# First embedding stage of a two-layer decoder trunk: two of four gate units as block products, inside the first MLP's pool

## The chip, the core and the metric

The kernel runs on one core of one Trainium2 chip. The metric is the device time of one execution in microseconds (us). It is the median of 3 runs. One further execution was recorded by the hardware profiler; all rows of "the profile" and "the trace" in this text are from it. The engines are PE (TensorE, matrix products), PEld (its weight loads), DVE (VectorE), ACT (ScalarE), POOL (GpSimd) and SP (which issues DMAs). L12 is line 12 of the kernel.

## What is computed

Two decoder layers over 512 tokens of width 1024, all in float32: a mixer (attention with a short convolution in layer 0, gated linear attention in layer 1), a gated MLP with a causal convolution, and the per-layer embedding. The change is in the embedding of layer 0:

```python
def _per_layer_embedding(x, p_i, norm, w_gate, w_proj):
    gate = jax.nn.sigmoid(_rms_norm(x, norm) @ w_gate)   # (512, 1024) @ (1024, 1024)
    return gate * (p_i @ w_proj)                         # (512, 256) @ (256, 1024)

for i in range(DEPTH):
    ...
    x = x + _conv_ffn(_rms_norm(x, ffn_norm[i]), ...)
    x = x + _per_layer_embedding(x, p[i], ple_norm[i], ple_w_gate[i], ple_w_proj[i])
```

## The kernel before, in words

**Tiles.** The residual `xT` lies turned: 8 tiles of 128 features x 512 tokens. Every float32 operand is split into a high part in the reduced format of TensorE and a low part (the rest), and each product is three matmuls (`mm3`, L162 to L164): high x high, high x low, low x high. `split` (L109/L110, or L112/L113 with a gain) does this for an operand, `cut` (L142/L143) for weights: ACT writes the high part, DVE subtracts. `advance` (L264) makes the next operand of a tile: split by the gain, square (L275), add to the sum of squares (L276). `end_norm` turns that sum with four PE transposes (L329), and DVE (L331, L171) and POOL (L172) make 1/rms; `spread` (L341) turns it into `R`, one row of 512 tokens on all partitions.

**Block products.** `seven` (L857) computes 256 output columns for 512 tokens by seven block products of 256 tokens where the plain way takes eight (a Strassen-Winograd scheme). A product is 4 block rows x 3 matmuls of 256 columns (L872 to L874). It is a generator with four steps: W, then ACT copies it into the two result banks X and Y (L883, L884); V, X left and Y left, then a copy (L893); X right, then ACT copies X right into Y right (L897); Y right and X right again. Its weight forms are made by `first_forms` and `more_forms` (four DVE subtractions of 512 columns in the loaded weights) and four `cut_blocks` (L819/L820). Its operand forms are sums of blocks of an even and an odd tile; in the MLP `operand` (L783) makes them (L791 scales by the gain, L796, L797, L800, L801 are the sums, then two splits). `seven` serves the MLPs of both layers.

**The stage.** `ple0` (L1281) runs in a pool of its own after the MLP of layer 0. It has four units of two output tiles. A unit loads 1 MB of gate weights and 256 KB of projection weights (both through L119 on SP), computes two gates of 48 matmuls in all (8 inputs x 3, for each tile), then for the unit before it two projections of `p` (12 matmuls), and `finish`: DVE multiplies gate and projection (L1295), adds to `xT` (L1296), and `advance` makes the operand for the mixer of layer 1. The gate itself is DVE times `R` (L1314), ACT sigmoid (L1315). The transposes of `end_norm`, `spread` and `load_p` (L1275) stand among the matmuls of unit 0. Right after the stage come the value products of the mixer of layer 1 (`Values`, 368 columns wide), then its first `feature` products.

**What sets the order.** A planner fixes the instruction order of each engine ahead of time: among what is ready in its reckoning, the earliest in the program goes first. Inside a `manual_schedule` block the instructions of the named engine keep the order of the program; ones from outside may fall between. Each engine then runs its list in order, waiting on semaphores. A pool keeps a fixed number of buffers for each tag. The tiles of a tag get theirs in the order of the program, each the first that is free; a buffer is free when the last instruction that uses its tile is done. In the MLP's pool there are 2 buffers of tag `zt` (`both()`, two halves of 512 columns each), 7 of `four`, 3 of `z`; elsewhere 3 of `wh` and `wl` (cut weights), 2 of `raw` (loaded weights), 4 banks `ps` and 4 `pa` of PSUM. A pool that reuses the memory of a closed one waits for all of that one.

Of the kernel before, what the change touches and what calls it, by code (L numbers as in the profile page):

```python
# [9 lines left out]
F32 = mybir.dt.float32  # L10
# [3 lines left out]
AF = mybir.ActivationFunctionType  # L14
ALU = mybir.AluOpType
# [3 lines left out]
P = 128  # L19
S = 512  # L20
D = 1024
NT = S // P
ND = D // P
# [5 lines left out]
ET = mybir.EngineType  # L29
# [27 lines left out]
class Kernel:  # L57
# [229 lines left out]
    def blocks(self, m, gain, scratch, tags):  # L287


        nc = self.nc  # L290
        H = S // 2
        gx = scratch()
        nc.scalar.activation(gx, self.xT[m], AF.Copy, scale=gain[:, m : m + 1])

        def parts(x):
            w = x.shape[1]
            h, l = self.pair(self.fp, *tags)
            self.split((h[:, :w], l[:, :w]), x)
            return lambda b, c: (h[:, b * H + c * P : b * H + (c + 1) * P], l[:, b * H + c * P : b * H + (c + 1) * P])

        if m % 2 == 0:
            self.even = gx
            self.e1 = parts(gx[:, :H])
        else:
            e, o = self.even, gx
            op = parts(o)
            s12, s34 = scratch(), scratch()
            nc.vector.tensor_tensor(s12[:, :H], e[:, H:], o[:, H:], ALU.add)
            nc.vector.tensor_tensor(s12[:, H:], s12[:, :H], e[:, :H], ALU.subtract)
            s12p = parts(s12)  # L310
            nc.vector.tensor_tensor(s34[:, :H], e[:, :H], e[:, H:], ALU.subtract)
            nc.vector.tensor_tensor(s34[:, H:], o[:, :H], s12[:, H:], ALU.subtract)
# [22 lines left out]
    def spread(self):  # L335
# [7 lines left out]
        nc.scalar.copy(R, pr)  # L343
        return R

# [437 lines left out]
    def operand(self, m, gain, tags):  # L783


        nc, fp = self.nc, self.mlp
        H = S // 2
        if m % 2 == 0:
            self.scratch = self.four(fp, F32)
        x = self.scratch[:, m % 2]  # L790
        nc.scalar.activation(x, self.xT[m], AF.Copy, scale=gain[:, m : m + 1])  # L791
        self.xg.append(self.pair(self.fp, *tags))
        self.split(self.xg[m], x)
        if m % 2:
            e, o, s12, s34 = (self.scratch[:, u] for u in range(4))
            nc.vector.tensor_tensor(s12[:, :H], e[:, H:], o[:, H:], ALU.add)  # L796
            nc.vector.tensor_tensor(s12[:, H:], s12[:, :H], e[:, :H], ALU.subtract)  # L797
            out = self.four(fp)
            self.split((out[:, 0], out[:, 1]), s12)
            nc.vector.tensor_tensor(s34[:, :H], e[:, :H], e[:, H:], ALU.subtract)  # L800
            nc.vector.tensor_tensor(s34[:, H:], o[:, :H], s12[:, H:], ALU.subtract)  # L801
            self.split((out[:, 2], out[:, 3]), s34)
            self.forms.append([(out[:, q, c], out[:, q + 1, c]) for q in (0, 2) for c in (slice(0, H), slice(H, S))])
        self.squares(m)

    def by_parity(self, raw):

# [49 lines left out]
    def seven(self, od, ws, xg, forms, keep=True):  # L857

        nc = self.nc
        H = S // 2
        mm = nc.tensor.matmul
        W, V = self.pa(), self.pa()[:, :H]
        X, Y = self.ps(), self.ps()
        plain, t13, t2 = ws

        def product(out, w, c, x, first=False):
            kw = dict(skip_group_check=True)
            for j in range(ND // 2):  # L870
                (wh, wl), (xh, xl) = w(j, c), x(j)
                mm(out, wh, xh, start=first and j == 0, stop=False, **kw)  # L872
                mm(out, wh, xl, start=False, stop=False, **kw)  # L873
                mm(out, wl, xh, start=False, stop=j == ND // 2 - 1, **kw)  # L874

        def tokens(u, half):
            c = slice(half * H, (half + 1) * H)
            return lambda j: (xg[2 * j + u][0][:, c], xg[2 * j + u][1][:, c])

        s1, s2, s3, s4 = (lambda j, q=q: forms[j][q] for q in range(4))  # L880
        left, right = slice(0, H), slice(H, S)
        product(W[:, left], plain, 0, tokens(0, 0), True)
        nc.scalar.copy(X[:, left], W[:, left])  # L883
        nc.scalar.copy(Y[:, left], W[:, left])  # L884
        yield
        product(V, t13, 0, s1, True)
        more = V
        if keep:
            more = self.sp.tile([P, S], F32, tag="acc", name=self.nm("more"), bufs=1)[:, :H]
            nc.scalar.copy(more, V)  # L890
        product(X[:, left], plain, 1, tokens(1, 0))
        product(Y[:, left], t2, 0, s2)
        nc.scalar.copy(X[:, right], Y[:, left])  # L893
        yield
        last = self.cut_blocks(od)
        product(X[:, right], t13, 1, s3)
        nc.scalar.copy(Y[:, right], X[:, right])  # L897
        yield
        product(Y[:, left], last, 1, s4)
        product(X[:, right], last, 0, tokens(1, 1))  # L900
        yield X, Y, more

    def ffn(self, i, project, next_gain):


        nc, a, tc = self.nc, self.a, self.tc
        gain = self.g_ffn[i]
        wu = a["ffn_w_up"][i].rearrange("(k p) n -> p k n", p=P)
        w0, w1, w2, bb = self.fcv

        mine, other = (("a0", "a1"), ("b0", "b1"))[:: 1 - 2 * i]
        with tc.tile_pool(name=f"ffn{i}", bufs=1) as fp:
# [4 lines left out]
            def both():  # L917
                return fp.tile([P, 2, S], F32, tag="zt", name=self.nm("zt"), bufs=2)
# [108 lines left out]
            xg = self.xg  # L1027
# [7 lines left out]
            steps, w1c, w0c = ready  # L1035
            with tc.manual_schedule(engines={ET.PE}):
                late = begin(0, steps, w1c)
                for d in range(groups):
                    g, y = both(), both()
# [7 lines left out]
                    if d == 0:  # L1047
                        R = self.spread()
                    X, Y, more = next(steps)
                    rest = late  # L1050

                    if d + 1 < groups:
                        steps, w1c, w0c = prepare(d + 1)
                        late = begin(d + 1, steps, w1c)
# [8 lines left out]
                    if 4 <= d < groups - 1:  # L1063
                        split_one(d - 4)
            self.begin_norm(mine)
            finish = lambda m: self.advance(m, next_gain)
            if i == 1:
                self.forms = []
                halves = []

                def half():
                    if not halves:
                        x = both()
                        halves.extend([x[:, 0], x[:, 1]])
                    return halves.pop(0)

                self.half = half
                finish = lambda m: self.blocks(m, next_gain, half, mine if m < 4 else other)
            work = [lambda f=f: split_blocks(f) for f in (14, 16, 18, 20)]
            for f in (8, 10, 12):  # L1080
                split_pair(f)
            self.down(i, acts, down_forms, both, work, finish)
            if i == 0:
                self.end_norm()
            else:
                self.ple1(fp)

    def down(self, i, acts, forms, both, work, finish):

# [188 lines left out]
            out.append(hl)  # L1278
        return out

    def ple0(self, next_gain):  # L1281
        nc, a = self.nc, self.a
        with self.tc.tile_pool(name="ple0", bufs=1) as pool:
            xg, R, pT = self.xg, None, None
            wg = a["ple_w_gate"][0].rearrange("(k p) n -> p k n", p=P)
            wp = a["ple_w_proj"][0].rearrange("(k p) n -> p k n", p=P)
            self.begin_norm(("b0", "b1"))

            def finish(m2, w, gates):
                for c in range(2):  # L1290
                    m, s = m2 + c, gates[c]
                    pj = self.ps()
                    for k in range(2):
                        self.mm3(pj, w(k, c * P, (c + 1) * P), pT[k], start=k == 0, stop=k == 1)
                    nc.vector.tensor_tensor(s, s, pj, ALU.mult)  # L1295
                    nc.vector.tensor_tensor(self.xT[m], self.xT[m], s, ALU.add)  # L1296
                    self.advance(m, next_gain)

            late = None
            for m2 in range(0, ND, 2):  # L1300
                g = self.weights(wg[:, :, m2 * P : (m2 + 2) * P], ND, 256)
                w = self.weights(wp[:, :, m2 * P : (m2 + 2) * P], 2, 256)
                gates = []
                for c in range(2):
                    pg = self.ps()
                    for k in range(ND):
                        self.mm3(pg, g(k, c * P, (c + 1) * P), xg[k], start=k == 0, stop=k == ND - 1)
                    gates.append(pg)
                if R is None:
                    R = self.spread()  # L1310
                    pT = self.load_p(0, pool)
                for c in range(2):
                    s = pool.tile([P, S], F32, tag="pg", name=self.nm("pg"), bufs=4)
                    nc.vector.tensor_tensor(s, gates[c], R, ALU.mult)  # L1314
                    nc.scalar.activation(s, s, AF.Sigmoid)  # L1315
                    gates[c] = s
                if late:
                    finish(*late)
                late = (m2, w, gates)
            finish(*late)  # L1320
            self.end_norm()

    def ple1(self, fp):
# [611 lines left out]
    def run(self):  # L1935
        self.setup()
        self.ffn(0, self.mixer0(), self.g_ple[0])
        self.ple0(self.g_mix[1])
        self.ffn(1, self.mixer1(), self.g_ple[1])


# [29 lines left out]
```

## Time and profile before

| | |
|---|---|
| median of 3 runs | 1207.76 us (1206.56 to 1208.12) |
| profiled execution | 1206.43 us, span 1204.7 us |
| busy share of the span | PE 99%, PEld 86%, DVE 80%, ACT 55%, POOL 4% |
| the stage on PE | 525.41 us (first gate matmul) to 581.68 us (first value matmul) |
| granted clock | 1.0 |

The busy share is that of all instructions of an engine in the span. A matmul's record overlaps the next one, so the pace of PE is read from the starts of consecutive rows, not from durations. Where a row of the timeline ends in brackets, the engine sat idle before it, and the arrow names what released it. A row with xN merges N instructions.

### The profile page before, as it was taken

Reading aid. Unit: us, or ns where it says so; the run is one execution under the profiler, and the core shown is the slowest. Engines: PE = TensorE matmul, PEld = TensorE weight load, DVE = VectorE, ACT = ScalarE, POOL = GpSimd, SP = SyncE. Lnnn points to the kernel's source line nnn. Section 1 sums busy time; section 2 is a strip of 40 time slices with the busy share of each in tenths; the row PEclk is TensorE's granted clock in tenths of the full one; section 3 lists DMA queues with packets and bytes.
Section 4 is the critical chain, followed back from the end, with each engine's and each line's share of the span. In section 5 each row is a group of like instructions: output and inputs, shape, how many; then the busy total and the mean of one; then the engine's idle time right before and its main releaser. Section 6 shows DMA issues by size and latency. Waiting matters only on the chain.

```text
span 1204.7 us, 17692 instructions
## 1 busy us (share of the span) xinstructions
PE 1197.7 (99%) x7013; PEld 1036.9 (86%) x7013; DVE 968.3 (80%) x1527; ACT 665.3 (55%) x1081; POOL 43.8 (4%) x64
## 2 busy tenths in 40 slices
PE   9999999999999999999999999999999999999998
PEld 8877788999899889888988988889998899888887
DVE  6786587899998986746579876677999999988595
ACT  7466455656555644534573564555565645646374
POOL 2600000000000000000100000000000000000000
PEclk9999999999999999999999999999999999999999
DMA  7321322423333242222322222313242423322501
GB/s 222 93 85 45 96 74 70 140 71 108 103 106 104 91 137 97 96 89 94 115 93 68 73 70 71 105 49 127 70 141 70 136 75 120 134 88 97 210 1 70
DMA packets 111127, 117.61 MB, mean 98 GB/s; under 512 B 2840, under 2 KB 106322, under 8 KB 111044
## 3 DMA queue, kind: packets, MB, share of 16 engines
q1 hardware_dynamic: 109680, 115.35, 29.2%
q8 instruction: 55, 0.90, 0.3%
q0 software_dynamic: 560, 0.42, 0.3%
q10 hardware_dynamic: 804, 0.70, 0.2%
q14 instruction: 28, 0.23, 0.1%
HBM read 114.37 MB, written 2.10 MB: 97 GB/s over the span
## 4 chain that ended last, share of the span: by engine, by line
PE 87%; DVE 8%; ACT 2%; issue 1%; POOL 1%; DMA 0%; ACTq 0%; DVEq 0%; POOLq 0%
PE ps L162 12%; PE ps L163 12%; PE ps L164 12%; PE pa L163 7%; PE pa L162 7%; PE pa L164 7%; PE ps L872 5%; PE ps L874 5%; PE ps L873 5%; PE pa L872 2%; PE pa L874 2%; PE pa L873 2%; DVE wl L143 2%; PE ps L1371 1%; PE ps L1369 1%
## 5 line engine op out<-in xcount | busy, mean ns | idle before, releaser
L142 ACT ACTIVATE wh<-raw 128x1024 fp32r<-128x1024 f32 (+4 forms) x154 | 152.4, 991 | 155.1 <-PE ps L163 109.4
L143 DVE TENSOR_TENSOR wl<-raw,wh 128x1024 fp32r<-128x1024 f32 (+4 forms) x154 | 175.6, 1142 | 50.1 <-ACT wh L142 49.7
L819 ACT ACTIVATE wh<-raw 128x1024 fp32r<-128x1024 f32 x78 | 82.8, 1061 | 118.4 <-DVE raw L844 65.2
L932 DVE SCALAR_TENSOR_TENSOR zt<-z,vfa,zt 128x510 f32<-128x510 f32 (+1 forms) x176 | 130.6, 744 | 11.7 <-ACT zt L930 11.2
L820 DVE TENSOR_TENSOR wl<-raw,wh 128x1024 fp32r<-128x1024 f32 x78 | 95.3, 1222 | 19.3 <-ACT wh L819 19.2
L930 ACT ACTIVATE zt<-z,vfb 128x512 f32<-128x512 f32 x88 | 71.1, 810 | 28.9 <-DVE four L983 12.8
L162 PE MATMUL ps<-b,wh 128*128 128x512 f32 x192 | 76.8, 400 | 0.0
L163 PE MATMUL ps<-b,wh 128*128 128x512 f32 x192 | 75.1, 391 | 0.0
L164 PE MATMUL ps<-b,wl 128*128 128x512 f32 x192 | 75.0, 391 | 0.0
L163 PE MATMUL pa<-b,wh 128*128 128x512 f32 x176 | 69.0, 392 | 0.0
L163 PE MATMUL pa<-a,wh 128*128 128x512 f32 x176 | 69.0, 392 | 0.0
L162 PE MATMUL pa<-a,wh 128*128 128x512 f32 x176 | 69.0, 392 | 0.0
L162 PE MATMUL pa<-b,wh 128*128 128x512 f32 x176 | 69.0, 392 | 0.0
L164 PE MATMUL pa<-a,wl 128*128 128x512 f32 x176 | 68.4, 389 | 0.0
L164 PE MATMUL pa<-b,wl 128*128 128x512 f32 x176 | 68.4, 389 | 0.0
L872 PE MATMUL ps<-four,wh 128*128 128x256 f32 x232 | 65.1, 281 | 0.5 <-ACT ps L893 0.5
L874 PE MATMUL ps<-four,wl 128*128 128x256 f32 x232 | 64.4, 278 | 0.0
L873 PE MATMUL ps<-four,wh 128*128 128x256 f32 x232 | 64.2, 277 | 0.0
L162 PE MATMUL ps<-a,wh 128*128 128x512 f32 x160 | 63.1, 394 | 0.0
L163 PE MATMUL ps<-a,wh 128*128 128x512 f32 x160 | 62.6, 392 | 0.0
L164 PE MATMUL ps<-a,wl 128*128 128x512 f32 x160 | 62.5, 391 | 0.0
L162 PE MATMUL ps<-uh,wh 128*128 128x512 f32 x128 | 50.3, 393 | 0.0
(475 smaller groups left out, 3491.5 us busy)
## 6 DMA issues: line engine op xcount, KB each, us to landing
raw<-in_ffn_w_up_dram SPq DMA_DIRECT2D x44, 1024.0 KB, 5.0
raw<-in_ffn_w_down_dram SPq DMA_DIRECT2D x13, 1024.0 KB, 4.8
raw<-in_hy_w_in_dram SPq DMA_DIRECT2D x8, 1024.0 KB, 5.1
raw<-in_gla_w_in_dram SPq DMA_DIRECT2D x8, 1024.0 KB, 5.1
raw<-in_ffn_w_down_dram SPq DMA_DIRECT2D x8, 768.0 KB, 4.1
raw<-in_ple_w_gate_dram SPq DMA_DIRECT2D x6, 1024.0 KB, 4.8
raw<-in_hy_w_out_dram SPq DMA_DIRECT2D x16, 256.0 KB, 4.2
raw<-in_gla_w_out_dram SPq DMA_DIRECT2D x4, 1024.0 KB, 4.8
```

Source lines behind the costliest of these rows:

```text
L142: nc.scalar.activation(hv, v, AF.Copy)
L143: nc.vector.tensor_tensor(lv, v, hv.bitcast(F32), ALU.subtract)
L162: mm(out, lh, rh, start=start, stop=False, **kw)
L163: mm(out, lh, rl, start=False, stop=False, **kw)
L164: mm(out, ll, rh, start=False, stop=stop, **kw)
L819: nc.scalar.activation(h, src, AF.Copy)
L820: nc.vector.tensor_tensor(l, src, h.bitcast(F32), ALU.subtract)
L872: mm(out, wh, xh, start=first and j == 0, stop=False, **kw)
L873: mm(out, wh, xl, start=False, stop=False, **kw)
L874: mm(out, wl, xh, start=False, stop=j == ND // 2 - 1, **kw)
L930: nc.scalar.activation(y, z, AF.Identity, scale=w2[:, f : f + 1], bias=bb[:, f : f + 1])
L932: nc.vector.scalar_tensor_tensor(out=y[:, tap:], in0=z[:, : S - tap], scalar=w[:, f : f + 1], in1=y[:, tap:], op0=ALU.mult, op1=ALU.add,)
```

## The change

`ple0` moves into the pool of the MLP of layer 0: `ffn` calls it with that pool, `end_norm` of the MLP goes into it, and its tiles use the tags of that pool. All PE instructions of the stage, the transposes and the last `end_norm` too, stand in one hand-ordered block. Units 0 and 1 stay plain. Units 2 and 3 become `seven`. The block sums of `operand` become a function of their own, `block_sums`, and the stage makes the four pairs of operand forms with it (`sums`), from `xT` and the gain. A pair takes four halves, so two buffers of `zt`: one for the two scaled tiles, one for the sums; the forms go to a buffer of `four`. The gates take a half each from the same two buffers. `sums(0)` stands after the sigmoids of gates 0 and 1, `sums(1)` to `sums(3)` after `finish` of tiles 0 and 1 and before the sigmoids of gates 2 and 3. The projection weights are loaded in one piece of 1 MB and split into two buffers of `four`, and a projection stands between the gates or after the first and the second step of `seven`. `p` comes through SP into two `z` tiles, early. V of `seven` is kept in a `z` tile, squares use `z` too. The lines of the old `ple0` are cut here.

```diff
--- before.py
+++ after.py
@@ -783,25 +783,32 @@
     def operand(self, m, gain, tags):
 
 
-        nc, fp = self.nc, self.mlp
-        H = S // 2
+        nc = self.nc
         if m % 2 == 0:
-            self.scratch = self.four(fp, F32)
-        x = self.scratch[:, m % 2]
+            four = self.four(self.mlp, F32)
+            self.scratch = [four[:, u] for u in range(4)]
+        x = self.scratch[m % 2]
         nc.scalar.activation(x, self.xT[m], AF.Copy, scale=gain[:, m : m + 1])
         self.xg.append(self.pair(self.fp, *tags))
         self.split(self.xg[m], x)
         if m % 2:
-            e, o, s12, s34 = (self.scratch[:, u] for u in range(4))
-            nc.vector.tensor_tensor(s12[:, :H], e[:, H:], o[:, H:], ALU.add)
-            nc.vector.tensor_tensor(s12[:, H:], s12[:, :H], e[:, :H], ALU.subtract)
-            out = self.four(fp)
-            self.split((out[:, 0], out[:, 1]), s12)
-            nc.vector.tensor_tensor(s34[:, :H], e[:, :H], e[:, H:], ALU.subtract)
-            nc.vector.tensor_tensor(s34[:, H:], o[:, :H], s12[:, H:], ALU.subtract)
-            self.split((out[:, 2], out[:, 3]), s34)
-            self.forms.append([(out[:, q, c], out[:, q + 1, c]) for q in (0, 2) for c in (slice(0, H), slice(H, S))])
+            self.forms.append(self.block_sums(self.scratch))
         self.squares(m)
+
+    def block_sums(self, rows):
+
+
+        nc = self.nc
+        H = S // 2
+        e, o, s12, s34 = rows
+        nc.vector.tensor_tensor(s12[:, :H], e[:, H:], o[:, H:], ALU.add)
+        nc.vector.tensor_tensor(s12[:, H:], s12[:, :H], e[:, :H], ALU.subtract)
+        out = self.four(self.mlp)
+        self.split((out[:, 0], out[:, 1]), s12)
+        nc.vector.tensor_tensor(s34[:, :H], e[:, :H], e[:, H:], ALU.subtract)
+        nc.vector.tensor_tensor(s34[:, H:], o[:, :H], s12[:, H:], ALU.subtract)
+        self.split((out[:, 2], out[:, 3]), s34)
+        return [(out[:, q, c], out[:, q + 1, c]) for q in (0, 2) for c in (slice(0, H), slice(H, S))]
 
     def by_parity(self, raw):
 
@@ -886,7 +893,7 @@
         product(V, t13, 0, s1, True)
         more = V
         if keep:
-            more = self.sp.tile([P, S], F32, tag="acc", name=self.nm("more"), bufs=1)[:, :H]
+            more = (keep() if callable(keep) else self.sp.tile([P, S], F32, tag="acc", name=self.nm("more"), bufs=1))[:, :H]
             nc.scalar.copy(more, V)
         product(X[:, left], plain, 1, tokens(1, 0))
         product(Y[:, left], t2, 0, s2)
@@ -1063,27 +1070,24 @@
                     if 4 <= d < groups - 1:
                         split_one(d - 4)
             self.begin_norm(mine)
+            halves = []
+
+            def half():
+                if not halves:
+                    x = both()
+                    halves.extend([x[:, 0], x[:, 1]])
+                return halves.pop(0)
+
+            self.half = half
             finish = lambda m: self.advance(m, next_gain)
             if i == 1:
                 self.forms = []
-                halves = []
-
-                def half():
-                    if not halves:
-                        x = both()
-                        halves.extend([x[:, 0], x[:, 1]])
-                    return halves.pop(0)
-
-                self.half = half
                 finish = lambda m: self.blocks(m, next_gain, half, mine if m < 4 else other)
             work = [lambda f=f: split_blocks(f) for f in (14, 16, 18, 20)]
             for f in (8, 10, 12):
                 split_pair(f)
             self.down(i, acts, down_forms, both, work, finish)
-            if i == 0:
-                self.end_norm()
-            else:
-                self.ple1(fp)
+            (self.ple1 if i else self.ple0)(fp)
 
     def down(self, i, acts, forms, both, work, finish):
 
@@ -1278,46 +1282,127 @@
             out.append(hl)
         return out
 
-    def ple0(self, next_gain):
...
+    def ple0(self, fp):
+        nc, a, tc = self.nc, self.a, self.tc
+        xg, forms = self.xg, []
+        wg = a["ple_w_gate"][0].rearrange("(k p) n -> p k n", p=P)
+        wp = a["ple_w_proj"][0].rearrange("(k p) n -> p k n", p=P)
+        units = ND // 2
+        def loaded(u):
+            raw = self.raw(ND, 2 * P)
+            nc.sync.dma_start(raw, wg[:, :, 2 * P * u : 2 * P * (u + 1)])
+            return raw
+        def sums(j):
+            rows = [self.half() for _ in range(4)]
+            for u in range(2):
+                m = 2 * j + u
+                nc.scalar.activation(rows[u], self.xT[m], AF.Copy, scale=self.g_ple[0][:, m : m + 1])
+            forms.append(self.block_sums(rows))
+        def square():
+            return fp.tile([P, S], F32, tag="z", name=self.nm("z"), bufs=3)
+        def sevens(u):
+            raw = loaded(u)
+            ev, od = self.by_parity(raw)
+            return self.seven(od, self.seven_forms(ev, od, raw), xg, forms, square)
+        def plain(w, c):
+            pg = self.ps()
+            for k in range(ND):
+                self.mm3(pg, w(k, c * P, (c + 1) * P), xg[k], start=k == 0, stop=k == ND - 1)
+            return pg
+        def projection():
+            raw = self.raw(2, D)
+            nc.sync.dma_start(raw, wp)
+            h, l = (self.four(fp).rearrange("p (k c) n -> p k (c n)", k=2) for _ in range(2))
+            for k in range(2):
+                nc.scalar.activation(h[:, k], raw[:, k], AF.Copy)
+                nc.vector.tensor_tensor(l[:, k], raw[:, k], h[:, k].bitcast(F32), ALU.subtract)
+            return h, l
+        def proj(m):
+            pj = self.ps()
+            c = slice(m * P, (m + 1) * P)
+            for k in range(2):
+                self.mm3(pj, (wph[:, k, c], wpl[:, k, c]), pT[k], start=k == 0, stop=k == 1)
+            return pj
+        def sigmoid(pg, more=None):
+            s = self.half()
+            if more is None:
+                nc.vector.tensor_tensor(s, pg, R, ALU.mult)
+            else:
+                h2 = lambda x: x.rearrange("p (u t) -> p u t", u=2)
+                nc.vector.tensor_tensor(h2(s), h2(pg), more.unsqueeze(1).to_broadcast([P, 2, S // 2]), ALU.add)
+                nc.vector.tensor_tensor(s, s, R, ALU.mult)
+            nc.scalar.activation(s, s, AF.Sigmoid)
+            return s
+        def finish(m, s, pj):
+            x = self.xT[m]
+            nc.vector.tensor_tensor(s, s, pj, ALU.mult)
+            nc.vector.tensor_tensor(x, x, s, ALU.add)
+            hl = self.pair(self.fp, "b0", "b1")
+            self.split(hl, x, self.g_mix[1][:, m : m + 1])
+            self.xg.append(hl)
+            if m == 0:
+                nc.scalar.activation(self.acc, x, AF.Square)
+            else:
+                sq = square()
+                nc.scalar.activation(sq, x, AF.Square)
+                nc.vector.tensor_tensor(self.acc, self.acc, sq, ALU.add)
+        src = a["p"][0, 0].rearrange("(t p) e -> p t e", p=P)
+        pin = [fp.tile([P, NT, P], F32, tag="z", name=self.nm("pin"), bufs=3) for _ in range(2)]
+        for e in range(2):
+            nc.sync.dma_start(pin[e], src[:, :, e * P : (e + 1) * P])
+        w = self.cut(loaded(0), "b")
+        with tc.manual_schedule(engines={ET.PE}):
+            gates = [plain(w, 0)]
+            self.end_norm()
+            w1 = self.cut(loaded(1), "b")
+            gates.append(plain(w, 1))
+            R = self.spread()
+            pT = self.load_p(0, fp, pin)
+            wph, wpl = projection()
             self.begin_norm(("b0", "b1"))
...
+            for u in range(1, units):
+                if u == 1:
+                    steps = sevens(2)
+                gates = [sigmoid(*((g,) if not isinstance(g, tuple) else g)) for g in gates]
+                m = 2 * u - 2
+                if u == 1:
+                    sums(0)
+                    new = [plain(w1, 0)]
+                    pjs = [proj(m)]
+                    new.append(plain(w1, 1))
+                    pjs.append(proj(m + 1))
+                else:
+                    next(steps)
+                    pjs = [proj(m)]
+                    next(steps)
+                    pjs.append(proj(m + 1))
+                    next(steps)
+                    X, Y, V = next(steps)
+                    new = [X, (Y, V)]
+                    if u + 1 < units:
+                        steps = sevens(u + 1)
                 for c in range(2):
...
+                    finish(m + c, gates[c], pjs[c])
+                for j in range(1, ND // 2 if u == 1 else 0):
+                    sums(j)
+                gates = new
+            gates = [sigmoid(*((g,) if not isinstance(g, tuple) else g)) for g in gates]
+            pjs = [proj(ND - 2 + c) for c in range(2)]
+            for c in range(2):
+                finish(ND - 2 + c, gates[c], pjs[c])
             self.end_norm()
 
     def ple1(self, fp):
@@ -1935,7 +2020,6 @@
     def run(self):
         self.setup()
         self.ffn(0, self.mixer0(), self.g_ple[0])
-        self.ple0(self.g_mix[1])
         self.ffn(1, self.mixer1(), self.g_ple[1])
```

35 lines of the change are left out of this document (removed).

## The prediction

> **What bounds the kernel now.** I read the page's first part, then the busy time of each engine in stretches around the stage, then the timeline of PE through it.
>
> ```profile
> span 1204.7 us, 17692 instructions
> PE 1197.7 (99%) x7013; PEld 1036.9 (86%) x7013; DVE 968.3 (80%) x1527; ACT 665.3 (55%) x1081; POOL 43.8 (4%) x64
> ```
>
> ```profile
> core 0: us, PE busy (x) PEld busy (x) DVE busy (x) ACT busy (x) POOL busy (x), PEclk, DMA share, GB/s
> 510.00:525.40 15.40, 15.40 (x69) 12.76 (x68) 4.59 (x6) 2.98 (x4) 0.00 (x0) 1.00 0.10 34
> 525.40:538.00 12.60, 12.60 (x64) 10.45 (x63) 6.18 (x11) 5.10 (x8) 1.01 (x1) 1.00 0.39 135
> 538.00:552.00 14.00, 14.00 (x65) 11.60 (x64) 7.39 (x11) 7.00 (x11) 0.00 (x0) 1.00 0.27 94
> 552.00:565.00 13.00, 13.00 (x59) 10.78 (x58) 8.14 (x12) 6.02 (x9) 0.00 (x0) 1.00 0.32 103
> 565.00:578.00 13.00, 13.00 (x59) 10.78 (x58) 8.87 (x14) 6.16 (x9) 0.00 (x0) 1.00 0.39 116
> 578.00:591.00 13.00, 13.00 (x73) 12.22 (x73) 12.96 (x21) 7.12 (x11) 1.97 (x5) 1.00 0.25 72
> ```
>
> PE is busy in every microsecond of the stage, also after it, where the mixer's value products cover the last `finish`. So a matmul taken out is worth its time, and every wait put into PE's list costs in full. DVE and ACT have room up to 578 us.
>
> **Fewer matmuls.** The pace is read from starts.
>
> ```profile
> 502.27 0.28 PE L872 MATMUL ps<-four,wh 128*128 128x256 f32 x1
> ...
> 503.63 0.40 PE L162 MATMUL ps<-four,wh 128*128 128x512 f32 x1
> ...
> 538.05 0.48 PE L162 MATMUL ps<-a,wh 128*128 128x512 f32 x1
> ...
> 549.04 0.39 PE L162 MATMUL ps<-ph,wh 128*128 128x512 f32 x1
> ...
> 551.53 0.39 PE L164 MATMUL ps<-ph,wl 128*128 128x512 f32 x1
> 551.76 0.39 PE L162 MATMUL ps<-a,wh 128*128 128x512 f32 x1
> ```
>
> From 502.27 one block product (12 matmuls of 256 columns) takes 1.36 us; seven take 9.5. A plain unit runs from 538.05 to 549.04, 11.0 us less 0.1 of refilling after a transpose: 10.9. Two units save 2 x 1.4 = **2.8 us**. Two projections take 551.76 - 549.04 = 2.72 us, 1.36 each; they are only moved. By 551.76 the old PE list has done units 0 and 1, all transposes and two projections. The new one does just the same before its first `seven`, so it also reaches W at 551.76 and the next projection at 551.76 + 1.36 = 553.1.
>
> **The wait for operand forms.** V needs the forms of all four pairs. Each pair takes two `zt` buffers, and there are two, which the gates use as well. Gates 0 and 1 come first in the program and hold one from the moment `R` is there until `finish` of tile 1 has added into `xT`, which needs projection 1. Pair 0 gets the second buffer for its scaled tiles but none for its sums. Only then can pair 0 go on, and pairs 1, 2, 3 follow one at a time. Gates 2 and 3 queue for `zt` behind pair 3; until they have read their `ps` banks, these stay taken, and with X and Y in the other two, the third projection has no bank. So PE stops ahead of that projection, all else in its list behind it (V, the later units, the last `end_norm`). Value products of the mixer may fall between, but lack weights: the `wh` buffers are held by unit 2 and next promised to unit 3.
>
> How long a pair takes is shown where the MLP makes the same sums, and the steps of gates and `finish` by these groups:
>
> ```profile
> 150.81 0.42 DVE L796 TENSOR_TENSOR four<-four 128x256 f32<-128x256 f32 x1
> 151.14 0.68 DVE L285 TENSOR_TENSOR acc<-acc,sq 128x512 f32<-128x512 f32 x1
> 151.74 0.69 DVE L110 TENSOR_TENSOR a<-four,a 128x512 fp32r<-128x512 f32 x1
> 152.34 0.42 DVE L797 TENSOR_TENSOR four<-four 128x256 f32<-128x256 f32 x1
> 152.80 0.42 DVE L801 TENSOR_TENSOR four<-four 128x256 f32<-128x256 f32 x1
> 153.46 1.29 DVE L110 TENSOR_TENSOR four<-four,four 128x512 fp32r<-128x512 f32 x2 [0.24 <-ACT four L109]
> ```
>
> ```profile
> L1314 DVE TENSOR_TENSOR pg<-ps,R 128x512 f32<-128x512 f32 x8 | 5.4, 688 | 15.1 <-PE ps L164 15.1
> L1295 DVE TENSOR_TENSOR pg<-pg,ps 128x512 f32<-128x512 f32 x8 | 5.3, 681 | 0.0
> L1296 DVE TENSOR_TENSOR xT<-xT,pg 128x512 f32<-128x512 f32 x8 | 5.2, 686 | 0.0
> L143 DVE TENSOR_TENSOR wl<-raw,wh 128x1024 fp32r<-128x1024 f32 x10 | 12.2, 1225 | 16.8 <-ACT wh L142 16.8
> ```
>
> From the first sum (150.81) to the last split (154.75) is 3.9 us with two foreign instructions between; without them (0.38, 0.46, 0.66 and 1.29 in a row) 2.8. The next pair's scaling runs beside the splits. I take 3.5, bounds 2.8 and 3.9. Projection 1 ends at 551.53 + 0.39 = 551.9; L1295 and L1296 take 1.4 (553.3); a cut of unit 2 (1.23 us) may stand in DVE's way, so between 553.3 and 554.6: I take 553.7. Three pairs: 10.5, to 564.2. Pair 3 gives its first buffer back after three sums: 1.3 to 2.4 us, taken 1.6, to 565.8. Gate 2 times `R`: 0.7, to 566.6 with latencies of 0.1. The stop is 566.6 - 553.1 = **13.5 us**, bounds 553.3 + 8.4 + 1.3 + 0.7 - 553.1 = 10.6, and 554.6 + 11.7 + 2.4 + 1.3 (gate behind another DVE instruction) - 553.1 = 16.9. The last pair's first split is done some 2 us after it frees that buffer, hidden behind the gate product (0.7) and the projection (1.36).
>
> **Hand-overs inside `seven`.** In the stage nothing stands between X right and Y right, which needs ACT's copy of X right (L897).
>
> ```profile
> 483.99 0.28 PE L874 MATMUL ps<-a,wl 128*128 128x256 f32 x1
> ...
> 484.24 1.06 ACT L142 ACTIVATE wh<-raw 128x1024 fp32r<-128x1024 f32 x1 [2.34 <-PE ps L873]
> ...
> 485.20 0.36 ACT L897 COPY ps<-ps 128x256 f32<-128x256 f32 x1
> ...
> 485.62 0.19 PEld L872 LDWEIGHTS ps<-a,wh 128*128 128x128 f32 x1 [0.40 <-ACT ps L897]
> ```
>
> Here other matmuls filled the gap. Without them PE waits the rest of the last matmul (0.28 - 0.11), the copy (0.36) and the start after it (0.06): 0.6 us, and 0.9 more where a cut stands first on ACT, as here (485.20 - 484.27). Twice that, and once for a `ps` bank at the start of unit 3 (gate 4, 0.6): 1.9 us, bounds 1.2 and 3.6.
>
> **The array after the stop.** This trace has no such stop on PE after its start; PE's longest wait, 1.3 us, is the first one:
>
> ```profile
> 1.32 3.35 PE L198 MATMUL pa<-ones_r 128*128 128x512 f32 x7 [1.32 <-DVE mhalf L186]
> ```
>
> Seven matmuls of 512 columns: (3.35 - 0.39) / 6 = 0.49 us apiece against 0.227 in the stage, 1.7 us lost on a start from rest, though the clock column says 1.00. I take these 1.7 us after the stop as well, bounds nothing and twice that, 3.4.
> [...]
>
> **At no cost.** Projection weights: four splits of 512 become two of 1024, on ACT and DVE, which have 5 us of 12.6 used by ACT and 6 by DVE before 538; p and the weights go through SP in loads of this kind:
>
> ```profile
> raw<-in_ple_w_gate_dram SPq DMA_DIRECT2D x6, 1024.0 KB, 4.8
> ```
>
> SP issues, in order: two of p, gate units 0 and 1, the projection, units 2 and 3, then the mixer's. Five microseconds each against 13.6 of PE per unit; the projection's buffer is free once unit 0 is cut, which gate 1 at 530.9 needs anyway; 4.8 to land and two cuts of 1.23 make 538.2 at the latest, before projection 0 at 543.5. Without that cover PE would wait the 7 us. The forms of units 2 and 3 add (3 x 1.23 + 5 x 0.68) - 2 x 1.23 = 4.6 us of DVE each. Unit 2's fit into DVE's idle 6.6 us of 538 to 552; unit 3's are done while PE works through unit 2. The four pairs' 12 us of DVE are the chain above, counted. The hand-placed last `end_norm` does not hold the value products, which may pass it. The mixer's pool now waits for all of the MLP's:
>
> ```profile
> POOL run L1836 <- DVE xT L1296: 54.4, 1, 54.4
> ```
>
> Already before, its first `memset` waits for the end of the stage, so this adds the 2 us from the last L1296 to the last square, under 12 us of value products.
>
> **Sum.** -2.8 + 13.5 + 1.9 + 1.7 = +14.3 us. Against the profiled execution: 1206.43 + 14.3 = 1220.7; the median lies 1.3 above that execution, so **1222 us**. Bounds: -2.8 + 10.6 + 1.2 + 0 = +9.0 (1217) and -2.8 + 16.9 + 3.6 + 3.4 = +21 (1229).
>
> **Rivals.**
> 1. *No slow start after the stop:* +12.6, 1220.4. For it: the clock column is 1.00 all through. Against it: the 0.49 us. Within the range.
> 2. *The sums are early* (the side of not slower): ACT and DVE are idle for 12 and 11 of the 15.4 us before 525.4, and by 508 tiles 0 to 5 are ready, with this addition of the MLP's last but one unit:
>
> ```profile
> 505.95 1.31 DVE L1181 TENSOR_TENSOR xT<-xT,ps 128x512 f32<-128x512 f32 x2
> ```
>
> If a buffer goes to whoever is ready first, or gates 0 and 1 leave theirs sooner, all pairs are done before V. It decides at 553.1 + 1.4 = 554.5: later, each microsecond is PE's. Then -2.8 + 1.9 = -0.9: 1206.9; with hand-overs at their lower bound 1206.2. Against it: the order of the program, in which gates 0 and 1 stand first in `zt`.
> 3. *DVE becomes the bound instead:* the buffers do not bind, but the stage holds 12.2 (four pairs of 4 x 0.42 + 2 x 0.69) + 2 x 4.6 + 2 x 0.7 = 23 us more DVE work. From 538 to 591 it is busy 7.39 + 8.14 + 8.87 + 12.96 = 37.4 of 53; with all of it 60, 7 over, some of which can go ahead of 538. That gives about +6: 1214.
>
> **How the numbers follow.** The forecast (a stop of 10.6 to 16.9 us and a slow start) has 0.6, rival 1 0.22, rival 2 0.1, rival 3 0.08. The first two lie in 1217 to 1229; for the pairs going quicker than their bound I open the lower end to 1216. Left out are rivals 2 and 3. A measurement can tell about 0.2%, 2.4 us. Rival 2 is mostly within that: same 0.08, faster 0.02 (saving 2.8 with free hand-overs); slower is the rest, 0.90.
>
> **What would show it.** One wait of PE of 11 to 17 us ahead of the third projection, released by DVE's gate product (or the last pair's sums), in a stage where DVE is not full; four rounds of block sums 3 to 4 us apart after projection 1; short waits for the L897 copy, two of them; matmuls of about twice 0.115 us after the long wait; 24 matmuls of 256 columns fewer than eight products would take. If the sums are found before 540 us, the step on buffers is wrong and rival 2 holds. If PE has many small waits, each for a cut or a sum on DVE, it is rival 3.

## The result and the profile after

The changed kernel takes 1225.01 us (median of 4 runs, 1224.30 to 1225.37); the kernel before, beside it, 1207.16 us (4 runs). The ratio is 1.0147, 95% interval [1.0135, 1.0159]: **1.5% slower**. The profiled execution took 1224.70 us, 18.27 more than that of before.

The first lines of the page of after; the last one is the clock that was granted, by slice:

```profile
span 1222.9 us, 17903 instructions
...
PE 1197.7 (98%) x7085; PEld 1039.2 (85%) x7085; DVE 990.8 (81%) x1563; ACT 680.3 (56%) x1109; POOL 44.2 (4%) x64
...
PEclk9999999999999999997999999999999999999999
```

PE's busy time is the same to the tenth, 1197.7 us, though its matmuls should need less: part of what was saved came back as slow matmuls (1.78 us, below). The rest of the loss is idle time. The waits of PE in after (us in total, times, longest):

```profile
PE ps L162 <- DVE zt L1340: 14.2, 2, 13.9
PE ps L879 <- ACT ps L904: 2.9, 2, 1.8
```

Where they lie, and what the matmuls behind them take, from the timeline of PE:

```profile
526.37 0.39 PE L162 MATMUL ps<-a,wh 128*128 128x512 f32 x1
...
553.93 0.28 PE L881 MATMUL pa<-a,wl 128*128 128x256 f32 x1
568.10 0.79 PE L162 MATMUL ps<-four,four 128*128 128x512 f32 x1 [13.90 <-DVE zt L1340]
568.70 0.63 PE L163 MATMUL ps<-four,four 128*128 128x512 f32 x1
569.12 0.63 PE L164 MATMUL ps<-four,four 128*128 128x512 f32 x1
...
570.83 0.41 PE L879 MATMUL pa<-four,wh 128*128 128x256 f32 x1
...
577.99 0.28 PE L881 MATMUL ps<-four,wl 128*128 128x256 f32 x1
580.06 0.39 PE L879 MATMUL ps<-four,wh 128*128 128x256 f32 x1 [1.80 <-ACT ps L904]
...
584.15 0.28 PE L881 MATMUL pa<-a,wl 128*128 128x256 f32 x1
584.72 0.50 PE L162 MATMUL ps<-four,four 128*128 128x512 f32 x1 [0.30 <-DVE zt L1340]
...
592.97 0.28 PE L881 MATMUL ps<-four,wl 128*128 128x256 f32 x1
594.31 0.38 PE L879 MATMUL ps<-four,wh 128*128 128x256 f32 x1 [1.06 <-ACT ps L904]
...
599.89 0.33 PE L162 MATMUL ps<-wh,b 128*128 128x368 f32 x1
```

The stage, from its first gate matmul to the first value product, lasts 599.89 - 526.37 = 73.52 us; before it was 581.68 - 525.41 = 56.27. Of the 18.27 us, 17.25 lie inside. They split as follows. An interval counts as lost time where the next start comes later than the pace of 0.114 us per 256 columns allows; the row behind a wait also takes about 0.11 longer to the next start (at 580.06 0.22 instead of 0.114).

| part | us | working |
|---|---|---|
| stop ahead of the third projection | +14.06 | 568.10 - 553.93 - 0.11 |
| slow matmuls behind it | +1.78 | projection 570.83 - 568.10 = 2.73 instead of 1.36; V 1.78 instead of 1.37 |
| two waits for L904, one for a bank | +3.98 | (1.96 + 0.11) + (1.23 + 0.11) + (0.46 + 0.11) |
| fewer matmuls | -2.72 | 24 matmuls of 256 columns, 0.1135 each |
| small losses elsewhere | +0.15 | the rest of 17.25 |

0.96 us more stand ahead of the stage (526.37 against 525.41). The twelve traces of this study start the stage between 525.06 and 526.82, and one that differs from after only behind that point (proj_later, below) starts it at 525.51, so I do not lay this on the change.

**The stop** is read on DVE. The timeline of DVE in after, cut to the instructions that set it:

```profile
554.27 0.69 DVE L1351 TENSOR_TENSOR xT<-xT,zt 128x512 f32<-128x512 f32 x1
555.00 0.43 DVE L804 TENSOR_TENSOR zt<-zt 128x256 f32<-128x256 f32 x1
...
559.00 0.43 DVE L808 TENSOR_TENSOR zt<-zt 128x256 f32<-128x256 f32 x1
...
562.31 0.42 DVE L808 TENSOR_TENSOR zt<-zt 128x256 f32<-128x256 f32 x1
...
565.64 0.42 DVE L808 TENSOR_TENSOR zt<-zt 128x256 f32<-128x256 f32 x1
...
567.36 0.69 DVE L1340 TENSOR_TENSOR zt<-ps,R 128x512 f32<-128x512 f32 x1
```

`finish` of tile 1 gives the buffer back at 554.96; the first block sum starts 0.04 us later, then a pair every 4.0, 3.3 and 3.3 us; 1.7 us after pair 3's first sum gate 2 is multiplied, and PE goes on.

### The profile page after: what moved, and what is told of

Its sections match the earlier page's. It is cut to its first block, busy times and chain, and to the rows that moved or that the text cites. A ratio compares the mean times of both kernels' runs of the same rounds, so it can differ in the third digit from the quotient of the medians.

```text
span 1222.9 us, 17903 instructions
## 1 busy us (share of the span) xinstructions
PE 1197.7 (98%) x7085; PEld 1039.2 (85%) x7085; DVE 990.8 (81%) x1563; ACT 680.3 (56%) x1109; POOL 44.2 (4%) x64
## 4 chain that ended last, share of the span: by engine, by line
PE 80%; DVE 13%; ACT 3%; issue 2%; DMA 1%; POOL 1%; SPq 0%; ACTq 0%; DVEq 0%; POOLq 0%
PE ps L162 11%; PE ps L163 11%; PE ps L164 11%; PE pa L163 6%; PE pa L162 6%; PE pa L164 6%; PE ps L879 5%; PE ps L881 5%; PE ps L880 5%; DVE wl L143 2%; PE pa L879 2%; PE pa L881 2%; PE pa L880 2%; DVE zt L939 2%; DVE wl L827 1%
## 5 line engine op out<-in xcount | busy, mean ns | idle before, releaser
L142 ACT ACTIVATE wh<-raw 128x1024 fp32r<-128x1024 f32 (+4 forms) x146 | 145.7, 999 | 137.0 <-PE ps L163 89.9
L143 DVE TENSOR_TENSOR wl<-raw,wh 128x1024 fp32r<-128x1024 f32 (+4 forms) x146 | 168.2, 1152 | 49.4 <-ACT wh L142 48.3
L826 ACT ACTIVATE wh<-raw 128x1024 fp32r<-128x1024 f32 x84 | 89.2, 1061 | 122.2 <-DVE raw L851 68.4
L827 DVE TENSOR_TENSOR wl<-raw,wh 128x1024 fp32r<-128x1024 f32 x84 | 102.6, 1222 | 22.5 <-ACT wh L826 22.5
L879 PE MATMUL ps<-four,wh 128*128 128x256 f32 x248 | 69.9, 282 | 3.6 <-ACT ps L904 2.9
L881 PE MATMUL ps<-four,wl 128*128 128x256 f32 x248 | 68.8, 278 | 0.0
L880 PE MATMUL ps<-four,wh 128*128 128x256 f32 x248 | 68.7, 277 | 0.0
L879 PEld LDWEIGHTS ps<-four,wh 128*128 128x128 f32 x248 | 46.5, 188 | 7.4 <-ACT ps L904 4.6
L162 PE MATMUL ps<-a,wh 128*128 128x512 f32 x128 | 50.6, 395 | 0.0
L163 PE MATMUL ps<-a,wh 128*128 128x512 f32 x128 | 50.2, 392 | 0.0
```

The source lines that it names most:

```text
L142: nc.scalar.activation(hv, v, AF.Copy)
L143: nc.vector.tensor_tensor(lv, v, hv.bitcast(F32), ALU.subtract)
L162: mm(out, lh, rh, start=start, stop=False, **kw)
L163: mm(out, lh, rl, start=False, stop=False, **kw)
L826: nc.scalar.activation(h, src, AF.Copy)
L827: nc.vector.tensor_tensor(l, src, h.bitcast(F32), ALU.subtract)
```

## The experiments

Each ratio is against the kernel before, run beside it on the same chip; its median was 1206.96 us for plain_all, sums_first, gates_z and warm, 1207.25 for four_early, gates_z_four, proj_later and both, 1206.50 for sums_mid_z and three. Differences between kernels of different groups are uncertain by these 0.75 us.

### plain_all: what else the change moved

All four units plain, no sums; the pool, the hand order, the early `p` and the projection in one piece stay.

```diff
-    steps = sevens(2)
+    ws = self.cut(loaded(2), "b")
...
-    sums(0)
...
-    next(steps)
+    new = [plain(ws, 0)]
     pjs = [proj(m)]
-    next(steps)
+    new.append(plain(ws, 1))
     pjs.append(proj(m + 1))
...
```

> The changed kernel with units 2 and 3 plain again and without block sums; the pool, the order by hand, the projection loaded at once and the loads through SP stay. Theory A: these cost nothing, 1207.2, or up to 1.0 more if the 0.96 us by which the changed kernel's stage starts later belongs to the change. Rival: the move into the pool and the order by hand cost by themselves, 1210 or more.

1207.38 us, ratio 1.0003 [0.9994, 1.0012]. Those parts cost nothing that can be told from no change; the whole loss belongs to the two units of block products and their sums.

### sums_first: the sums ahead of everything in the stage

```diff
+    for j in range(ND // 2):
+        sums(j)
     with tc.manual_schedule(engines={ET.PE}):
...
-    sums(0)
...
-    for j in range(1, ND // 2 if u == 1 else 0):
-        sums(j)
```

> The changed kernel with all four pairs of block sums placed ahead of the gates in the program, so that they get the two zt buffers first; everything else, DVE's work included, is the same. Theory A: no stop ahead of the third projection, 1209.1, between 1207.5 and 1211; what is left against before are the hand-overs (3.9) less the saved matmuls (2.4). Theory B: the work has to be done all the same, 1215 or more.

1210.65 us, ratio 1.0032 [1.0021, 1.0043], inside the range of theory A and below that of B: 14.4 us of the 17.9 are gone by program order alone, with the same work. The first form's low part is there at 505 us (DVE), and PE's longest wait in the stage is 2.4 us, for the bank of the fifth projection:

```profile
504.83 0.68 DVE L110 TENSOR_TENSOR four<-zt,four 128x512 fp32r<-128x512 f32 x1
```

```profile
569.22 0.50 PE L162 MATMUL ps<-four,four 128*128 128x512 f32 x1 [2.36 <-DVE zt L1340]
```

### gates_z: only the sharing of zt undone

```diff
 def sigmoid(pg, more=None):
-    s = self.half()
+    s = square()
```

> The changed kernel with the gates in buffers of tag z instead of halves of zt; program order unchanged. Theory A (the two zt buffers, shared with the gates and handed out in program order, make the stop of 14.1 us, and the restart of the array after it costs 1.8): both go, 1225.0 - 15.9 = 1209.1, between 1208 and 1211; the block sums are found before 540 us. Theory B (the stop is the sums' own 12 us of DVE work, which has no room): the sums still end after 560, the stop stays above 8 us, 1218 or more.

1219.40 us, ratio 1.0100 [1.0086, 1.0114]: 5.6 us less than after, in the range of theory B, and **theory A missed by 10**. Taking the gates out of `zt` was not enough. The trace shows where they stood. Pair 0 is summed at 505.76 now (DVE), yet its first split waits until 544.51 (ACT), and not for lack of time on ACT, which idles 5.45 us ahead of 538.25:

```profile
505.76 0.42 DVE L809 TENSOR_TENSOR zt<-zt,zt 128x256 f32<-128x256 f32 x1
```

```profile
538.25 0.58 ACT L343 COPY R<-pa 128x512 f32<-128x512 f32 x1 [5.45 <-PE pa L341]
538.74 1.10 ACT L109 ACTIVATE four<-pa 128x512 fp32r<-128x512 f32 x2
539.70 2.02 ACT L1326 ACTIVATE four<-raw 128x1024 fp32r<-128x1024 f32 x2
...
544.51 0.61 ACT L109 ACTIVATE four<-zt 128x512 fp32r<-128x512 f32 x1
```

The form goes into a buffer of `four`, and in the program `p` and the two projection buffers stand ahead of it in that tag; `p` needs PE's transposes and writes at 538.74. From there on DVE is full:

```profile
core 0: us, PE busy (x) PEld busy (x) DVE busy (x) ACT busy (x) POOL busy (x), PEclk, DMA share, GB/s
...
540.00:555.00 15.00, 14.10 (x69) 11.71 (x67) 14.94 (x24) 11.24 (x16) 0.00 (x0) 1.00 0.21 72
555.00:570.00 15.00, 9.54 (x48) 8.25 (x49) 13.66 (x26) 10.77 (x18) 0.00 (x0) 0.77 0.17 50
```

So two readings were open: a second tag in program order, or the volume of DVE's work from 540 us on.

### four_early and gates_z_four: buffers taken early by name

Both take four buffers of `four` ahead of `p`'s and hand them to the sums; the second also has the edit of gates_z.

```diff
...
+    early = [self.four(fp) for _ in range(ND // 2)]
...
-    forms.append(self.block_sums(rows))
+    forms.append(self.block_sums(rows, early[j]))
```

> The four buffers of tag four for the sums' forms are taken before those of p and of the projection weights; the gates still share zt with the sums. Theory A (two tags handed out in program order, zt by the gates and four by p and the projection; either one alone holds the sums back): zt still binds, the sums still run one pair after another after the first finish, PE's stop stays at 13 to 15 us, 1223 to 1227 us. Rival C (the order of tag four is what holds the sums, zt counts little): the stop shrinks below 8 us and the time to 1211 to 1219.

> As four_early, and the gates' sigmoids take z tiles, so neither tag holds the sums. Theory A: the sums run ahead of 540 us and the time comes near that of all sums placed first, 1208 to 1212 us. Rival B (the volume of DVE's work from 540 to 568 us sets the end, whoever holds the buffers): 1216 to 1220, as with the z tiles alone.

1225.03 us, 1.0146 [1.0131, 1.0162], and 1219.76 us, 1.0105 [1.0092, 1.0119]. Neither figure decides anything: the order of the instructions on every engine is the same as without the edit. So a tile that is only named takes no place. The reading that was left, a tile takes its buffer where the program first writes it, is what the next kernel tests. The two runs are repetitions of after and of gates_z.

### sums_mid_z: the sums first to write, zt not shared

The gates' sigmoids use `z`, and the sums stand behind those of gates 0 and 1, but ahead of `load_p` and `projection`.

```diff
     R = self.spread()
+    gates = [sigmoid(g) for g in gates]
+    for j in range(ND // 2):
+        sums(j)
     pT = self.load_p(0, fp, pin)
...
```

> The gates' sigmoids take z tiles, and in the program all four sums stand behind those of gates 0 and 1 but ahead of the operand p and of the projection weights, so that their forms are the first to write buffers of tag four. (Taking those buffers by name earlier, without writing, changed nothing in the order of the engines, so the two runs on that were no test.) Theory A (a tag's buffers go out in the order in which the program first writes them; with zt free it is four, first written at 538 us by p, that held the forms back): first form before 530 us, 1208 to 1212 us. Rival B (DVE's volume from 540 to 568 us, wherever the sums stand): 1216 to 1220 us.

1212.41 us, ratio 1.0046 [1.0034, 1.0059]: 7.0 us less than gates_z, 0.4 above theory A's range, far from theory B's. The first form's low part is written at 504.21 us (DVE), the last pair's from 533.07 us on, all ahead of `p`:

```profile
533.07 1.28 DVE L110 TENSOR_TENSOR four<-zt,four 128x512 fp32r<-128x512 f32 x2
```

DVE's volume is the same in both kernels; only its place moved. The 2.4 and 1.5 us that PE still waits here for the gates' products (L1340) were not followed further. The same order with `zt` shared would block itself, by the order of the buffers (the gates would keep `zt` until a projection that needs a buffer of `four` behind the sums' own); it was not run.

### warm: the clock

58 matmuls of 512 columns into a bank that nobody reads, just ahead of the third projection.

```diff
+    if u == 2:
+        d = self.pa()
+        for _ in range(58):
+            nc.tensor.matmul(d, xg[0][0][:, :P], xg[0][0], start=True, stop=True)
     pjs = [proj(m)]
```

> The changed kernel with 58 matmuls of 512 columns of no use (13.2 us, into a bank that nobody reads) ahead of the third projection, so that PE works through most of the stop. If the slow pace after the stop is the array's restart: the stop stays (third projection at about 568), the projection takes 1.36 instead of 2.73 and V 1.37 instead of 1.78: 1223.2. If the slow pace has another cause (operands that come late, a port shared with DVE): 1225.0 as the changed kernel.

1223.88 us, ratio 1.0137 [1.0123, 1.0151]. PE is busy 13.05 of 13.70 us through the stop; behind it the projection is back to 0.23 us per matmul:

```profile
core 0: us, PE busy (x) PEld busy (x) DVE busy (x) ACT busy (x) POOL busy (x), PEclk, DMA share, GB/s
553.50:567.20 13.70, 13.05 (x58) 10.46 (x56) 12.63 (x27) 10.05 (x18) 0.00 (x0) 1.00 0.18 55
567.20:571.00 3.80, 3.71 (x26) 3.45 (x27) 3.21 (x6) 1.90 (x5) 0.00 (x0) 1.00 0.00 0
```

```profile
567.29 0.50 PE L162 MATMUL ps<-four,four 128*128 128x512 f32 x1 [0.74 <-DVE zt L1340]
567.63 0.39 PE L163 MATMUL ps<-four,four 128*128 128x512 f32 x1
```

It was idleness that made the matmuls slow: with PE kept busy the same projection and V, at the same place behind the same sums, have their pace back. The median gains 1.1 us. In the trace the stage is 1.31 us shorter, and three things make that up: of the 1.78 us of slow matmuls 0.18 are left; the wait for L1340 in unit 3 grows from 0.30 to 1.55 us; and the first hand-over costs 1.06 instead of 2.07 us, because on ACT the copy L904 (576.22) stands ahead of the cut (576.49) here.

### proj_later: the hand-overs

```diff
     next(steps)
+    next(steps)
     pjs = [proj(m)]
     next(steps)
     pjs.append(proj(m + 1))
-    next(steps)
     X, Y, V = next(steps)
```

> Each projection of a seven stands one step later, so that the second one (1.36 us) lies between X right and Y right, where PE waited 1.95 and 1.2 us for ACT's copy L904. Theory A (the hand-over is a wait in PE's list, and a product in between covers it): 1.2 to 2.6 us less than 1225.0, 1222.4 to 1223.8. Rival (the wait goes elsewhere, to the bank or the gate behind it): 1224.5 to 1225.5.

1221.68 us, ratio 1.0116 [1.0102, 1.0130]: 3.3 us less than after, 0.7 more than the most expected. No wait for L904 is left in the stage. The stop changes its form as well: V, whose bank is free, now stands ahead of the projection and takes each pair as it comes. By the starts of the trace, stop and slow matmuls together cost 0.9 us less for that, so not all of the gain is the hand-overs.

```profile
555.95 0.39 PE L879 MATMUL pa<-four,wh 128*128 128x256 f32 x1 [2.61 <-ACT four L109]
...
566.74 0.58 PE L879 MATMUL pa<-four,wh 128*128 128x256 f32 x1 [1.80 <-ACT four L109]
```

### both and three: the two repairs together, and one unit more

both is sums_first with proj_later, edit for edit. three makes unit 1 a `seven` too:

```diff
-    w1 = self.cut(loaded(1), "b")
+    steps = sevens(1)
...
-    if u == 1:
-        steps = sevens(2)
...
-    if u == 1:
-        new = [plain(w1, 0)]
-        pjs = [proj(m)]
-        new.append(plain(w1, 1))
-        pjs.append(proj(m + 1))
-    else:
...
```

> All four sums placed ahead of the gates, and each projection of a seven one step later. Theory A (stop and hand-overs are the two costs of the change): 1210.65 less 1.2 to 2.6, that is 1208.0 to 1209.5 us, within 0.2% of the kernel before (1207.0); if the 2.4 us wait for a bank goes as well, 1206. Rival (DVE and ACT, with all this work in 525 to 580 us, are late somewhere else): 1210 or more.

> Sums first and projections one step later, and unit 1 as block products too. Theory A (now only the matmuls count): 12 matmuls of 256 columns less than with two such units, 1.36 us, and one or two short waits more: 1204.0 to 1205.5. Rival (unit 1's forms and cuts, 4.6 us of DVE ahead of 538 us beside the sums, and V at 540 us are late): 1206 to 1211.

both: 1205.64 us, ratio **0.9988 [0.9979, 0.9997]**, less than theory A's range, since the wait for the bank went too (1206 was given for that), and with it the slow matmuls that followed it in sums_first (last section). PE's one wait in the stage that the trace names:

```profile
563.09 0.39 PE L879 MATMUL ps<-four,wh 128*128 128x256 f32 x1 [0.21 <-ACT ps L904]
```

The stage takes 54.20 us in the trace, 2.07 less than before: the 2.72 of fewer matmuls, less 0.6 of waits. It is the only version that beats the kernel before; 1.6 us or 0.13% by the medians is below the 0.2% that the prediction called measurable, though the interval leaves 1 out.

three: 1208.82 us, ratio 1.0017 [1.0008, 1.0026], 3.2 us more than both by the medians, in the rival's range, but not by the cause it named. In the traces its stage is 2.5 us longer: one wait of 2.71 us takes more than the 1.36 of the twelve matmuls. In seven of its eleven executions the granted clock was lower as well (last section). The rows of PE and ACT:

```profile
545.02 0.39 PE L879 MATMUL ps<-a,wh 128*128 128x256 f32 x1 [2.71 <-ACT ps L890]
```

```profile
540.76 2.00 ACT L1326 ACTIVATE four<-raw 128x1024 fp32r<-128x1024 f32 x2
542.78 1.28 ACT L1345 ACT_TABLE_LOAD   x1
544.07 0.63 ACT L1345 ACTIVATE zt<-zt 128x512 f32<-128x512 f32 x1
544.61 0.37 ACT L890 COPY ps<-pa 128x256 f32<-128x256 f32 x1
```

The copy of W queues on ACT behind the cut of the projection weights, the load of the sigmoid's table and the first sigmoid.

## Why the prediction was right, and where it was off

**Forecast.** 1222 us predicted, 1225.01 measured, within 1216 to 1229; slower, as forecast at 0.9. In its own sum +14.3 against +17.25 in the stage. The range held although one term, the hand-overs, left its own bounds; the bounds of the others left room for it.

**Fewer matmuls, -2.8:** -2.72.

**The stop, 13.5:** 14.06, by the chain that was given. Counted from the same point (the stage starts 0.96 later), `finish` of tile 1 ends at 554.0 for the 553.7 taken; from pair 0's first sum to pair 3's 10.64 us for 10.5; pair 3's buffer 1.7 for 1.6. sums_first shows that order is the cause. But as an account of *why the sums could not go earlier* the step was incomplete. It named `zt` alone, and rival 2 said that all pairs would be done before V if gates 0 and 1 left theirs sooner. gates_z gave 1219.4 there, not 1206.9. `four` holds the forms as well, behind `p`; `zt` only came last. That 5.6 us go with `zt` and 7.0 more with the place in front of `p` is measured; that the latter is the buffer and not some other effect of the moved lines rests on the idle ACT at 538 us.

**The array after the stop, 1.7:** 1.78, and warm shows the cause. Rival 1 (no slow start) is refuted.

**Hand-overs, 1.9, bounds 1.2 to 3.6:** 3.98. This is the term that was mis-sized, by more than its upper bound (and three times its 0.6 is 1.8, not 1.9). The mechanism stood in the prediction with its price: 0.6 us, and 0.9 more where a cut stands first on ACT, as in the very row that it quoted. I took the short price twice; both times a cut was there. The two cost 2.07 and 1.34 us, the wait for the bank 0.57, of which 0.11 each is the longer first row that the price left out. The first cut itself came late, having waited 2.79 us for a sum of weight blocks on DVE (L851), while X right had ended at 578.27; that put it above the long price. ACT in after:

```profile
578.68 1.06 ACT L826 ACTIVATE wh<-raw 128x1024 fp32r<-128x1024 f32 x1 [2.79 <-DVE raw L851]
579.64 0.37 ACT L904 COPY ps<-ps 128x256 f32<-128x256 f32 x1
...
593.16 0.82 ACT L142 ACTIVATE wh<-raw 128x736 fp32r<-128x736 f32 x1 [2.29 <-PE ps L880]
593.89 0.37 ACT L904 COPY ps<-ps 128x256 f32<-128x256 f32 x1
```

The short price itself was close. In sums_first no cut stands ahead of the first copy on ACT, and from the last matmul of X right (561.69) to Y right it is 0.78 us, 0.67 more than the pace (0.94 more in warm, where the copy is ahead of the cut as well):

```profile
562.47 0.38 PE L879 MATMUL ps<-four,wh 128*128 128x256 f32 x1 [0.50 <-ACT ps L904]
```

proj_later confirms that these waits were PE's own time: a product in between hides them.

**At no cost:** right for what plain_all holds, the pool, the order by hand, `p` and the projection weights. The weight forms of the two units are not in that kernel, and those of unit 3 came late enough to hold up the first hand-over. **Rival 3** (DVE is the bound): sums_mid_z and both do the same DVE work without the loss; it is no bound, as long as the work can start ahead of 540 us. The sign that was named against it, a stage where DVE is not full, did not show: DVE was busy 14.41 of the 15.5 us of the stop (window below), with the sums themselves. Only the runs tell the two apart.

Open: the 0.96 us ahead of the stage, and why the median of sums_mid_z lies 0.4 us above theory A's range. Its trace cannot say, since the profiled execution took 1210.81 us, inside the range; of its five executions the two with a granted clock of 1.000 took 1210.81 and 1211.69, the three with less 1212.41 to 1213.28.

## What to carry to other kernels

A new step that shares buffers with an existing one stands in the queue of every tag it writes, at the place where the program first writes each; put work whose inputs are ready early (the block sums) early in the text, and check all its tags, since freeing one only shows the next. Price a PE to ACT to PE hand-over with what stands in front of the copy in ACT's list, not with the copy alone, and lay an independent product in the gap. A saving of 2.7 us in matmuls is soon eaten: here two such queues turned it into 17 us lost, and with both removed 1.6 us were left.

## What the runs showed of the hardware

The clock column shows the stop. It had read 1.00 for the slow start that the prediction took from PE's first row. In the windows of after:

```profile
core 0: us, PE busy (x) PEld busy (x) DVE busy (x) ACT busy (x) POOL busy (x), PEclk, DMA share, GB/s
...
552.50:568.00 15.50, 1.70 (x14) 1.47 (x12) 14.41 (x29) 10.10 (x18) 0.00 (x0) 0.68 0.17 49
568.00:572.00 4.00, 3.90 (x13) 3.32 (x14) 2.68 (x6) 1.31 (x3) 0.00 (x0) 0.55 0.00 0
```

Behind the 13.9 us of rest a matmul of 512 columns takes 0.43 us from start to start instead of 0.227, until about 571.5, some 3.4 us. Single matmuls do not keep the pace up here: in proj_later PE gets three matmuls of each pair during the stop, and the ten behind them still start 0.21 us apart, where 0.114 is the pace. From the timeline of PE:

```profile
568.45 0.41 PE L879 MATMUL ps<-a,wh 128*128 128x256 f32 x1
568.67 0.41 PE L880 MATMUL ps<-a,wh 128*128 128x256 f32 x1
```

A shorter wait can bring the slow pace too. In sums_first PE waits 2.36 us ahead of the fifth projection (569.22). The first matmuls behind it keep their pace; from 570.48 to 573.89, 3.4 us, they take nearly twice as long, and 1.7 us are lost. That is less rest than the 13.9 us in after, and the slow stretch is as long:

```profile
570.90 0.41 PE L879 MATMUL pa<-four,wh 128*128 128x256 f32 x1
571.12 0.41 PE L880 MATMUL pa<-four,wh 128*128 128x256 f32 x1
```

The length of the wait alone does not decide it: behind waits of 2.38 us in sums_mid_z and 2.71 us in three, the profiled executions show no such stretch. What decides it was not tested. It fits that executions of one kernel differ where such a wait stands: three took 1207.00 to 1207.95 us in the four with a granted clock of 1.000, 1208.50 to 1210.54 us in the seven with 0.997 to 0.999. both, which has no such wait, shows no such split.
